# Turning q and k on VectorE and through HBM instead of on TensorE, in one encoder block on one core

## The chip, the core and the metric

The kernel runs on one NeuronCore of one Trainium2 chip. The metric is the device time of one execution in microseconds (us), lower is better. TensorE (PE in the profile, with its weight load PEld), VectorE (DVE), ScalarE (ACT) and GpSimd (POOL) each work through their own list of instructions in order; SyncE (SP) issues transfers. GpSimd issues transfers too. An instruction that waits holds up all that stand behind it on its engine.

## The reference

One layer of a bidirectional encoder, x of 512 tokens by 1024 features, float32. The tokens are a grid of 8 rows by 64 columns.

```python
x = x + 0.5 * swiglu1(rmsnorm(x))                    # 1024 -> 2 * 2816 -> 1024
h = rmsnorm(x)
xr, gr, q, k, v, ga, gb = split(h @ w_in)            # seven times 1024 columns
# A: depthwise conv of xr, two RG-LRU scans (forward, backward), summed, times gelu(gr)
q = rmsnorm(q per head, q_norm) * 64 ** -0.5         # 16 heads of 64
k = rmsnorm(k per head, k_norm)
s = q @ k^T + rel_pos_bias in a window of 8 rows x 16 columns   # -inf outside
B = softmax(s) @ v
x = x + (sigmoid(ga) * A + sigmoid(gb) * B) @ w_out
x = x + 0.5 * swiglu2(rmsnorm(x))
```

## The kernel before

**Layout.** The residual lies with features on partitions: eight tiles of 128 features by 512 tokens. Tokens are ordered by four column blocks of 16 columns, in each of them 8 rows of 16. Every product is made of three float32r matmuls (high times high, high times low, low times high): a weight tile of 128x1024 comes in on SP (`load_w`, L159), ACT rounds it to its high part (L145) and DVE subtracts to get the low part (L148). Three raw buffers and four pairs of high and low parts let the loads run ahead of TensorE.

**Stages.** The first feed-forward runs to about 330 us, the xr projection and the convolution follow, then q, k and v (`tok_group`, L822, tokens on partitions, in two halves of eight heads), the three gate projections (`gates`, L1070), the output projection (L1114) and the second feed-forward.

**What runs between.** The attention and the recurrence are written as generators in lanes (`lanes`, L574): `att` and `tail` hold attention, `lru` the recurrence, `v` the gathers of V. `weave(rate)` (L577) advances each lane by its rate of `RATE` (L83) at fixed places of the projections. The rates in the gate stage are "g". A scheduler of the language then sets each engine's order; `hold` (L251) ties an instruction behind the last projection matmul issued at that place, as an order and not as a wait.

**q and k.** For each half, `qk_raw` (L838) leaves four tiles of q and four of k, tokens on partitions, and the sums of squares per head. `heads` (L896) turns the sums into inverse norms (L901, L903, L904), multiplies them in (L909) and then, in `start(fi)` for each of four groups of two heads, turns q and k to features on partitions by eight TensorE transposes against `ident` (L918, L920). ACT evicts q and k with the norm weights as scale (L924, L927), DVE makes the low parts (L926, L929).

**Scores and softmax.** `scores` (L933) makes 12 matmuls for each group and half of the column blocks (24 where both halves go together, in the second half). DVE adds the bias and takes the maximum (L970), ACT takes the exponent and the row sum (L977), DVE inverts the sum (L979) and multiplies it in (L982). `ship` (L985) turns the probabilities in 32x32 blocks on DVE (L991, L992), writes them to HBM on SP (`pd`, L994) and reads them back rearranged by four GpSimd transfers (`PT`, L998). `apply` (L1001) multiplies by V.

**V.** `v_get` (L852) writes V to HBM (`vd`, L860). `v_more` (L866) gathers what is shifted against the column blocks: three `vs` tiles (L869) and, for the two edge blocks, `va` and `ve` in twelve GpSimd transfers (L880). The first half's gathers are issued at once, the second half's advance with lane `v` at 0.25. `bm` tiles (L892) are the bias, on GpSimd as well.

Of the kernel before, what the change touches and what calls it, by code (L numbers as in the profile page):

```python
# [9 lines left out]
F32 = mybir.dt.float32  # L10
F32R = mybir.dt.float32r
AF = mybir.ActivationFunctionType
ALU = mybir.AluOpType
# [3 lines left out]
P = 128  # L17
# [9 lines left out]
NCB, QC = 4, 16  # L27
# [16 lines left out]
C_QN, C_KN = 112, 113  # L44
# [39 lines left out]
    "xr": {"att": 0.0, "lru": 2.75},  # L84
    "t0": {"att": 0.0, "lru": 3.25},
    "t1": {"att": 0.75, "tail": 0.75, "lru": 2},
    "g": {"att": 0.7, "tail": 0.7, "lru": 1.5, "v": 0.25},
}


# [1 line left out]
def block_kernel(ctx: ExitStack, tc, a, out):  # L92
    nc = tc.nc
# [7 lines left out]
    dram = ctx.enter_context(tc.tile_pool(name="dram", bufs=1, space=bass.MemoryType.DRAM))  # L101
# [4 lines left out]
    mark = {}  # L106

    def nm(s):
        uid[0] += 1
        return f"{s}_{uid[0]}"  # L110
# [3 lines left out]
    def big_t(dt=F32, shape=(P, T), n="b"):  # L114
        return big.tile(list(shape), dt, tag="big", bufs=NBIG, name=nm(n))
# [4 lines left out]
    def acc_t():  # L120
        return acc.tile([P, T], F32, tag="acc", name=nm("acc"))

    def aux_t():
        return aux.tile([P, T], F32, tag="aux", name=nm("aux"))


    small = const.tile([P, NSMALL], F32, name="small")
# [4 lines left out]
    ident = const.tile([P, P], F32, name="ident")  # L132
# [118 lines left out]
    def hold(i):  # L251

        after(i, mark["mm"])
        return i
# [316 lines left out]
        end(t1, o)  # L571


    lanes = {"att": [], "tail": [], "lru": [], "v": []}  # L574
    due = {"att": 0.0, "tail": 0.0, "lru": 0.0, "v": 0.0}

    def weave(rate):  # L577
        for ln, n in rate.items():
# [11 lines left out]
    def until(ln, done):  # L590
        while lanes[ln] and not done():
            weave({ln: 1.0})
# [63 lines left out]
    ab = const.tile([P, 16], F32, name="ab")  # L656
# [21 lines left out]
    nc.vector.tensor_scalar(sn8, sp, -8.0, None, ALU.mult)  # L678
    gq8 = const.tile([P, 1], F32, name="gq8")
    nc.vector.tensor_scalar(gq8, small[:, C_QN : C_QN + 1], HD**-0.5, None, ALU.mult)  # L680
    gk = small[:, C_KN : C_KN + 1]

    state = {}

    def perm(ap):

        return ap.rearrange("p (r j c) -> p j r c", r=ROWS, j=NCB)
# [150 lines left out]
    def qk_raw(w, hf, st):  # L838
        raws = []
        for ps in tok_group(w, hf):  # L840
            t = big_t(n="qk")
            with tc.high_priority():
                copy = nc.scalar.activation(t, ps, AF.Copy)
            raws.append(t)
        for j, t in enumerate(raws):
            sq = big_t(n="sq")
            after(nc.scalar.activation(sq, t, AF.Square), copy)
            nc.vector.reduce_sum(st[:, w, j, :], sq.rearrange("p (h d) -> p h d", d=HD), axis=AX.X)
        weave(RATE[phase[0]])
        return raws  # L850

    def v_get(hf):  # L852
        for j, ps in enumerate(tok_group(2, hf)):
            t = big_t(n="v")
            with tc.high_priority():
                nc.vector.tensor_scalar(t, ps, rcol[:, j : j + 1], None, ALU.mult)
            V[hf, 2 * j] = t

        for j in range(NCB):
            nc.sync.dma_start(vd[hf][:, j * QC : (j + 1) * QC, :], V[hf, 2 * j])  # L860
        lanes["v"].append(v_more(hf))
        if hf == 0:
            until("v", lambda: False)
        weave(RATE[phase[0]])
# [28 lines left out]
            if g == 0:  # L893
                after(ld, mark["xr"])

    def heads(hf, raws, st):  # L896

        rq = tiny.tile([P, 2, NCB, 8], F32, tag="rq", name=nm("rq"))
        for w in range(2):
# [6 lines left out]
        for w in range(2):  # L906
            for j in range(NCB):
                t = raws[w][j].rearrange("p (h d) -> p h d", d=HD)
                hold(nc.vector.tensor_tensor(t, t, rq[:, w, j, :].unsqueeze(2).to_broadcast([P, 8, HD]), ALU.mult))  # L909
            yield  # L910
        qk, rss, soft, PTs = {}, {}, {}, {}


        def start(fi):
            fs = slice(fi * P, (fi + 1) * P)
            pq, pk = aux_t(), aux_t()
            for j in range(NCB):
                hold(nc.tensor.transpose(pq[:, j * P : (j + 1) * P], raws[0][j][:, fs], ident))  # L918
            for j in range(NCB):
                hold(nc.tensor.transpose(perm(pk)[:, j], raws[1][j][:, fs], ident))  # L920
            rev = lambda t: t.rearrange("p (j t) -> p j t", j=NCB)[:, :, ::-1]
            fwd = lambda t: t.rearrange("p (j t) -> p j t", j=NCB)
            qh, ql, kh, kl = (big_t(F32R, n=n) for n in ("qh", "ql", "kh", "kl"))
            nc.scalar.activation(rev(qh), fwd(pq), AF.Copy, scale=gq8)  # L924
            with tc.high_priority():
                nc.vector.scalar_tensor_tensor(rev(ql), fwd(pq), gq8, rev(qh.bitcast(F32)), ALU.mult, ALU.subtract)  # L926
            nc.scalar.activation(kh, pk, AF.Copy, scale=gk)  # L927
            with tc.high_priority():
                mark["kl"] = nc.vector.scalar_tensor_tensor(kl, pk, gk, kh.bitcast(F32), ALU.mult, ALU.subtract)  # L929
            grid = lambda t: t.rearrange("p (r c) -> p r c", r=ROWS)  # L930
            qk[fi] = qh, ql, grid(kh), grid(kl)

        def scores(fi, n2s):  # L933

            qh, ql, kh, kl = qk[fi]
            if 0 in n2s:
                rss[fi] = tiny.tile([P, 2, NCB], F32, tag="rs", name=nm("rs"))
            rs = rss[fi]
            pss = {n2: [aux_t() if n2 == n2s[0] else acc_t() for _ in range(2)] for n2 in n2s}
            for n in [n2 * 2 + i for n2 in n2s for i in range(2)]:  # L940
                ps, i = pss[n // 2], n % 2
                if n in EDGE:
                    keys = lambda t: t[:, :, SSTART[n] : SSTART[n] + 2 * QC].rearrange("p r (g c) -> p g r c", c=8)
                else:
                    keys = lambda t: t[:, :, KSTART[n] : KSTART[n] + 2 * QC].rearrange("p r (h c) -> p h r c", h=2)
                cs = slice(i * 256, (i + 1) * 256)
                for q_, k_ in ((qh, kl), (qh, kh), (ql, kh)):
                    for hp in (1, 0):
                        o = slice(hp * HD, (hp + 1) * HD)
                        mm = hold(nc.tensor.matmul(  # L950
                            ps[hp][:, cs], q_[o, n * P : (n + 1) * P], keys(k_[o]),
                            start=k_ is kl, stop=q_ is ql))
            for n2 in n2s:

                soft[fi, n2] = big_t(n="p"), big_t(n="p")
            for n2, hp in [(n2, hp) for n2 in n2s for hp in range(2)]:
                ps = pss[n2]
                bm = bms[hf * 4 + fi, hp]
                so = big_t(n="so")
                nmx = tiny.tile([P, 2], F32, tag="nmx", bufs=4, name=nm("nmx"))  # L960
                parts = []
                for i in range(2):
                    n = n2 * 2 + i
                    w = BIAS[n].stop - BIAS[n].start
                    pt = soft[fi, n2][n not in EDGE][:, hp * w : (hp + 1) * w]
                    parts.append(pt)
                    so_ = so[:, i * 256 : i * 256 + w]
                    o = i * 256 + (ROWS * (KSTART[n] - SSTART[n]) if n in EDGE else 0)
                    with tc.high_priority():
                        nc.vector.tensor_tensor_reduce(  # L970
                            so_, ps[hp][:, o : o + w], bm[:, BIAS[n]],
                            -1.0, 3.0e38, ALU.add, ALU.min, nmx[:, i : i + 1])
                    if n in EDGE and hp == (n == 0):

                        pt, so_ = (t.rearrange("p (g k) -> p g k", k=G) for t in (pt, so_))
                        pt = pt[:, ::-1]
                    nc.scalar.activation(pt, so_, AF.Exp, scale=-1.0, bias=nmx[:, i : i + 1],  # L977
                                         accum_out=rs[:, hp, n : n + 1])
                nc.vector.reciprocal(rs[:, hp, n2 * 2 : n2 * 2 + 2], rs[:, hp, n2 * 2 : n2 * 2 + 2])  # L979
                for i, pt in enumerate(parts):  # L980
                    n = n2 * 2 + i
                    nc.vector.tensor_scalar(pt, pt, rs[:, hp, n : n + 1], None, ALU.mult)  # L982
            return mm

        def ship(fi, n2):  # L985
# [73 lines left out]
    att = [None] * KT  # L1059
    phase = ["t0"]  # L1060
    bias(0)
    for hf in range(2):
        st = tiny.tile([P, 2, NCB, 8], F32, tag="st", name=nm("st"))
        raws = [qk_raw(0, hf, st), qk_raw(1, hf, st)]
        v_get(hf)
        lanes["att"].append(heads(hf, raws, st))
        phase[0] = "t1" if hf == 0 else "g"


# [144 lines left out]
```

## Time and profile before

| what | value |
|---|---|
| two runs | 1114.73 and 1115.2 us, median 1114.97 |
| the profiled execution | 1114.18 us |
| its span | 1112.4 us |
| mean granted TensorE clock | 0.997 |
| busy: PE, PEld, DVE, ACT, POOL | 1100.6, 974.8, 813.2, 578.0, 149.3 us |

The span is what the profile's time axis covers; some 1.8 us lie around it. Busy time is per engine and overlaps. A line such as "PE L918 MATMUL aux<-ident,qk x4" names the engine, the line of the kernel, the operation and the tiles by the program's names; in the time line "[4.72 <-DMA va<-vd]" is idle time ahead of the instruction and what ended it. "issue" means a wait for nothing that the profile shows.

### The profile page before, as it was taken

To read this page: it belongs to the slowest core of one execution; us is meant where nothing else is said; L and a number is where in the kernel's file an instruction comes from. 1 tells how busy PE (TensorE), PEld (TensorE's weight loads), DVE (VectorE), ACT (ScalarE), POOL (GpSimd) and SP (SyncE) were. 2 spreads that over 40 slices of the span, in tenths; PEclk is the share of its full clock that TensorE was granted. 3 is DMA by queue.
4 is the path that set the end of the run, shared out by engine and by line. 5 is a ranking of instruction groups with operands and counts; after the bars stand their busy time and mean duration, and the time that the engine had idled before them with its cause. 6 is when DMAs were issued, how large, how long until landed. Compare 5 with 4: busy or idle time off the path is not lost.

```text
span 1112.4 us, 17673 instructions
## 1 busy us (share of the span) xinstructions
PE 1100.6 (99%) x6811; PEld 974.8 (88%) x6811; DVE 813.2 (73%) x1295; ACT 578.0 (52%) x871; POOL 149.3 (13%) x243
## 2 busy tenths in 40 slices
PE   9999999999999999999999979999999999999998
PEld 8899999988888778788888868889999999998887
DVE  7878777794745776999877956759877777785542
ACT  8554544563533679877454432346554454564330
POOL 0000000000000351230333542001000000000000
PEclk9999999999999999999999989999999999999999
DMA  8566666643423685573687655377766666553421
GB/s 267 153 169 152 150 156 167 159 147 95 133 82 107 168 255 152 167 210 106 211 260 184 195 176 160 104 239 160 199 146 158 157 166 147 157 170 95 133 76 38
DMA packets 64548, 175.93 MB, mean 158 GB/s; under 512 B 14544, under 2 KB 18384, under 8 KB 64464
## 3 DMA queue, kind: packets, MB, share of 16 engines
q1 hardware_dynamic: 43136, 127.75, 35.5%
q0 software_dynamic: 20752, 46.80, 21.0%
q8 instruction: 53, 0.87, 0.3%
q10 hardware_dynamic: 576, 0.26, 0.1%
q14 instruction: 31, 0.25, 0.1%
HBM read 150.53 MB, written 15.73 MB: 149 GB/s over the span
## 4 chain that ended last, share of the span: by engine, by line
PE 95%; issue 1%; DMA 1%; DVE 1%; POOL 1%; ACT 0%; ACTq 0%; POOLq 0%
PE acc L312 31%; PE acc L172 10%; PE acc L173 10%; PE acc L174 10%; PE aux L312 5%; PE acc L831 4%; PE acc L832 4%; PE acc L833 4%; PE aux L174 4%; PE aux L172 4%; PE aux L173 4%; PE aux L742 1%; PE aux L1013 1%; PE aux L950 1%; PE acc L464 1%
## 5 line engine op out<-in xcount | busy, mean ns | idle before, releaser
L145 ACT ACTIVATE wh<-wraw 128x1024 fp32r<-128x1024 f32 (+3 forms) x224 | 220.3, 988 | 304.2 <-issue 95.0
L148 DVE TENSOR_TENSOR wl<-wraw,wh 128x1024 fp32r<-128x1024 f32 (+3 forms) x236 | 267.0, 1136 | 100.1 <-ACT wh L145 98.8
L312 PE MATMUL acc<-s,wh 128*128 128x256 f32 x1280 | 232.2, 283 | 0.0
L312 PEld LDWEIGHTS acc<-s,wh 128*128 128x128 f32 x1280 | 199.7, 192 | 0.0
L312 PE MATMUL acc<-s,wl 128*128 128x256 f32 x640 | 181.1, 283 | 0.0
L312 PEld LDWEIGHTS acc<-s,wl 128*128 128x128 f32 x640 | 122.9, 192 | 0.0
L172 PE MATMUL acc<-xh,wh 128*128 128x512 f32 x272 | 107.5, 395 | 0.0
L174 PE MATMUL acc<-xh,wl 128*128 128x512 f32 x272 | 106.2, 391 | 0.0
L173 PE MATMUL acc<-xl,wh 128*128 128x512 f32 x272 | 106.1, 390 | 0.0
L312 PE MATMUL acc<-xl,wh 128*128 128x256 f32 x320 | 90.6, 283 | 0.0
L312 PE MATMUL acc<-xh,wl 128*128 128x256 f32 x320 | 90.6, 283 | 0.0
L312 PE MATMUL acc<-xh,wh 128*128 128x256 f32 x320 | 90.5, 283 | 0.0
L831 PE MATMUL acc<-wh,xh 128*128 128x512 f32 x192 | 75.7, 394 | 0.0
L832 PE MATMUL acc<-wh,xl 128*128 128x512 f32 x192 | 74.8, 389 | 0.0
L833 PE MATMUL acc<-wl,xh 128*128 128x512 f32 x192 | 74.8, 389 | 0.0
L148 DVE TENSOR_TENSOR hl<-h,hh 128x512 fp32r<-128x512 f32 x88 | 57.2, 687 | 21.7 <-PE aux L173 21.5
L172 PE MATMUL aux<-hh,wh 128*128 128x512 f32 (+1 forms) x181 | 69.9, 386 | 0.0
L173 PE MATMUL aux<-hl,wh 128*128 128x512 f32 (+1 forms) x181 | 69.9, 386 | 0.0
L174 PE MATMUL aux<-hh,wl 128*128 128x512 f32 (+1 forms) x181 | 69.9, 386 | 0.0
L174 PE MATMUL acc<-hh,wl 128*128 128x512 f32 (+1 forms) x176 | 67.9, 386 | 0.0
L173 PE MATMUL acc<-hl,wh 128*128 128x512 f32 (+1 forms) x176 | 67.9, 386 | 0.0
L172 PE MATMUL acc<-hh,wh 128*128 128x512 f32 (+1 forms) x176 | 67.9, 386 | 0.0
(221 smaller groups left out, 2297.6 us busy)
## 6 DMA issues: line engine op xcount, KB each, us to landing
wraw<-wqkv SPq DMA_DIRECT2D x24, 512.0 KB, 4.5
wraw<-wg SPq DMA_DIRECT2D x24, 512.0 KB, 7.4
wraw<-w1d SPq DMA_DIRECT2D x22, 512.0 KB, 3.7
wraw<-w2s SPq DMA_DIRECT2D x22, 512.0 KB
pair<-w2s SPq DMA_DIRECT2D x22, 512.0 KB, 4.4
wraw<-w2d SPq DMA_DIRECT2D x22, 512.0 KB, 3.6
wraw<-w1s SPq DMA_DIRECT2D x18, 512.0 KB, 3.5
pair<-w1s SPq DMA_DIRECT2D x18, 512.0 KB, 4.7
```

The costliest lines, as they stand in the source:

```text
L145: nc.scalar.activation(H, raw, AF.Copy)
L148: return nc.vector.tensor_tensor(L, raw, H.bitcast(F32), ALU.subtract)
L172: nc.tensor.matmul(ps, wh, xh, start=first, stop=False, skip_group_check=skip)
L173: nc.tensor.matmul(ps, wh, xl, start=False, stop=False, skip_group_check=skip)
L174: mark["mm"] = nc.tensor.matmul(ps, wl, xh, start=False, stop=last, skip_group_check=skip)
L312: mm = nc.tensor.matmul(o, w_[:, c], x_, start=first and m + k == 0 and w_ is H and x_ is xh_, stop=m + k == 4 and w_ is L, skip_group_che ...
L464: nc.tensor.matmul(pre[i], w[i][1][:, s], xh[k], start=k == 0, stop=False)
L742: prev, mm = mm, nc.tensor.matmul(ps[d][b], W[w][o, c], X[x][o], start=x == 1, stop=w + x == 0)
L831: nc.tensor.matmul(pss[j], xh[kk][:, tj], H[:, s], start=kk == 0, stop=False)
L832: nc.tensor.matmul(pss[j], xl[kk][:, tj], H[:, s], start=False, stop=False)
L833: mark["mm"] = nc.tensor.matmul(pss[j], xh[kk][:, tj], L[:, s], start=False, stop=kk == KT - 1)
L950: mm = hold(nc.tensor.matmul(ps[hp][:, cs], q_[o, n * P : (n + 1) * P], keys(k_[o]), start=k_ is kl, stop=q_ is ql))
```

## The change

- **q and k are turned without TensorE.** `turn_qk` takes over the norm and its product. After the product, each of the eight tiles of a half is turned by one DVE `transpose` in 32x32 blocks into a tile `qkt`, and four GpSimd transfers write it to a tensor `qd` in HBM, 32x4 runs of 512 bytes each: 32 transfers a half. `heads` reads it back with `fetch(fi)` on SP, one transfer for q and one for k for each group, 128x16 runs of 128 bytes each. The loads for the next group are issued in `start`. The eight TensorE transposes of `start` are gone; ACT and DVE read the fetched tile in SBUF instead of PSUM. k_norm is folded into the scale of q.
- **The second half's turn is in a lane of its own**, `prep`, which advances at 0.25 in the gate stage; `heads` first empties it.
- **The inverse row sum is multiplied in by ACT** (an activation with a scale) instead of DVE.
- **Lane `v` advances at 0.5** in the gate stage instead of 0.25.

```diff
-    "g": {"att": 0.7, "tail": 0.7, "lru": 1.5, "v": 0.25},
+    "g": {"att": 0.7, "tail": 0.7, "lru": 1.5, "v": 0.5, "prep": 0.25},
...
-    def heads(hf, raws, st):
+    def turn_qk(raws, st, qd):
...
                 hold(nc.vector.tensor_tensor(t, t, rq[:, w, j, :].unsqueeze(2).to_broadcast([P, 8, HD]), ALU.mult))
-            yield
+                t2 = big_t(n="qkt")
+                nc.vector.transpose(
+                    t2.rearrange("p (c f i) -> p f c i", c=NCB, i=32), raws[w][j].rearrange("p (f c i) -> p f c i", c=NCB, i=32))
+                for ab in range(NCB):
+                    nc.gpsimd.dma_start(
+                        qd[w].rearrange("(c i) j a x -> j a i c x", c=NCB)[j, ab],
+                        t2[ab * 32 : (ab + 1) * 32].rearrange("p (c x) -> p c x", c=NCB))
+                if j % 2 == 1:
+                    yield
+
+    def heads(hf, qd):
+
+        xs = {}
+
+        def fetch(fi):
+            for w in range(2):
+                xs[w, fi] = big_t(n="xqk")
+                nc.sync.dma_start(
+                    xs[w, fi].rearrange("p (x i) -> p x i", i=32),
+                    qd[w].rearrange("p j a (f i) -> f p (j a) i", i=32)[fi])
+
+        until("prep", lambda: False)
+        fetch(0)
+        yield
...
-            pq, pk = aux_t(), aux_t()
-            for j in range(NCB):
-                hold(nc.tensor.transpose(pq[:, j * P : (j + 1) * P], raws[0][j][:, fs], ident))
-            for j in range(NCB):
-                hold(nc.tensor.transpose(perm(pk)[:, j], raws[1][j][:, fs], ident))
+            if fi < 3:
+                fetch(fi + 1)
+            xq, xk = (xs.pop((w, fi)).rearrange("p (j a i) -> p j a i", j=NCB, i=32) for w in range(2))
...
-            nc.scalar.activation(rev(qh), fwd(pq), AF.Copy, scale=gq8)
+            hold(nc.scalar.activation(rev(qh), xq, AF.Copy, scale=gq8))
...
-                    nc.vector.tensor_scalar(pt, pt, rs[:, hp, n : n + 1], None, ALU.mult)
+                    nc.scalar.activation(pt, pt, AF.Copy, scale=rs[:, hp, n : n + 1])
...
-        lanes["att"].append(heads(hf, raws, st))
+        lanes["att" if hf == 0 else "prep"].append(turn_qk(raws, st, qd))
+        lanes["att"].append(heads(hf, qd))
```

On TensorE, before, at the first group of the first half: eight transposes (L918 of q, L920 of k) between two stretches of the v projection (L831 to L833).

```order
L833 MATMUL acc_5122<-wl_5158,xh_3094 128x512
L918 MATMUL aux_5186<-ident,qk_4440 128x128
L918 MATMUL aux_5186<-ident,qk_4442 128x128
L918 MATMUL aux_5186<-ident,qk_4444 128x128
L918 MATMUL aux_5186<-ident,qk_4446 128x128
L920 MATMUL aux_5187<-ident,qk_4625 128x8x16
L920 MATMUL aux_5187<-ident,qk_4627 128x8x16
L920 MATMUL aux_5187<-ident,qk_4629 128x8x16
L920 MATMUL aux_5187<-ident,qk_4631 128x8x16
L831 MATMUL acc_5119<-wh_5207,xh_3096 128x512
```

On TensorE, now, at the first scores of the second half (L971 is the score matmul, kl_6382 and qh_6379 come from the first group that is fetched for that half):

```order
L172 MATMUL acc_6356<-xh_3102,wh_6358 128x512
L173 MATMUL acc_6356<-xl_3103,wh_6358 128x512
L174 MATMUL acc_6356<-xh_3102,wl_6359 128x512
L971 MATMUL aux_6402<-kl_6382,qh_6379 128x256
L971 MATMUL aux_6401<-kl_6382,qh_6379 128x256
L971 MATMUL aux_6402<-kh_6381,qh_6379 128x256
L971 MATMUL aux_6401<-kh_6381,qh_6379 128x256
L971 MATMUL aux_6402<-kh_6381,ql_6380 128x256
L971 MATMUL aux_6401<-kh_6381,ql_6380 128x256
```

No transposes are left. Counted in the order from the end of the last recurrence gates (L742) on, 312 projection matmuls now precede the first scores of the first half (216 before), and 600 precede the first scores of the second half (528 before).

On GpSimd, before, between the last probabilities of the first half and V's edges of the second (PT, bm, vs, va and ve as above, vd_82 is the second half's V):

```order
L998 DMA PT_5901<-pd_5899 128x1x224 x4
L892 DMA bm_6325<-rpb 128x640
L869 DMA vs_6018<-vd_82 128x1x512
L892 DMA bm_6327<-rpb 128x640
L869 DMA vs_6111<-vd_82 128x1x512
L998 DMA PT_6013<-pd_6011 128x1x224 x4
L892 DMA bm_6540<-rpb 128x640
L892 DMA bm_6542<-rpb 128x640
L876 MEMSET ve_6330 128x512
L880 DMA va_6329<-vd_82 64x4x64 x2
L880 DMA ve_6330<-vd_82 64x4x64
```

On GpSimd, now, the end of the same stretch; qd_5323 and qd_5324 are q and k of the second half, L1019 reads the probabilities back:

```order
L914 DMA qd_5323<-qkt_6056 32x4x128 x2
L914 DMA qd_5323<-qkt_6063 32x4x128 x4
L892 DMA bm_6133<-rpb 128x640
L892 DMA bm_6135<-rpb 128x640
L880 DMA va_6049<-vd_82 64x4x64 x2
L880 DMA ve_6050<-vd_82 64x4x64
L1019 DMA PT_6128<-pd_6126 128x1x224 x4
L914 DMA qd_5324<-qkt_6249 32x4x128 x4
L914 DMA qd_5324<-qkt_6256 32x4x128 x4
L1019 DMA PT_6243<-pd_6241 128x1x224 x4
L914 DMA qd_5324<-qkt_6326 32x4x128 x4
L914 DMA qd_5324<-qkt_6333 32x4x128 x4
```

The 32 writes of the second half's q and k stand among the first half's probabilities and the second half's V gathers; the last of them stand behind all eight groups of PT of the first half. V's edges of the second half, which stood behind all PT of the first half, now stand among them. From the first PT on to the last write of qd there are 32 transfers of PT, 32 of qd, 12 of va and ve, 3 of vs and 4 of bm.

On SP, now, at the second half's fetches (xqk):

```order
L163 DMA wraw_6945<-wg 128x1024
L1015 DMA pd_6241<-pt_6238 128x896
L163 DMA wraw_6977<-wg 128x1024
L927 DMA xqk_6339<-qd_5323 128x16x32
L927 DMA xqk_6341<-qd_5324 128x16x32
L927 DMA xqk_6375<-qd_5323 128x16x32
L927 DMA xqk_6377<-qd_5324 128x16x32
L927 DMA xqk_6489<-qd_5323 128x16x32
L1015 DMA pd_6472<-pt_6469 128x896
L927 DMA xqk_6491<-qd_5324 128x16x32
L1015 DMA pd_6482<-pt_6479 128x896
L163 DMA wraw_7117<-wg 128x1024
```

The fetches stand between the 18th and the 19th weight tile of the gate projections, and wait for all writes of qd.

More of the change, by code (lines that the diff above doesn't have):

```diff
@@ L571, in ffn @@
         end(t1, o)
-    lanes = {"att": [], "tail": [], "lru": [], "v": []}
-    due = {"att": 0.0, "tail": 0.0, "lru": 0.0, "v": 0.0}
+    lanes = {"att": [], "tail": [], "lru": [], "v": [], "prep": []}
+    due = {"att": 0.0, "tail": 0.0, "lru": 0.0, "v": 0.0, "prep": 0.0}
     def weave(rate):
@@ L680, in block_kernel @@
     nc.vector.tensor_scalar(gq8, small[:, C_QN : C_QN + 1], HD**-0.5, None, ALU.mult)
-    gk = small[:, C_KN : C_KN + 1]
+    nc.vector.tensor_tensor(gq8, gq8, small[:, C_KN : C_KN + 1], ALU.mult)
     state = {}
@@ L911, in heads @@
+                if j % 2 == 1:
[11 more added lines that the diff above has]
+        yield
         qk, rss, soft, PTs = {}, {}, {}, {}
         def start(fi):
-            fs = slice(fi * P, (fi + 1) * P)
@@ L916, in start @@
-            pq, pk = aux_t(), aux_t()
-            for j in range(NCB):
-                hold(nc.tensor.transpose(pq[:, j * P : (j + 1) * P], raws[0][j][:, fs], ident))
-            for j in range(NCB):
-                hold(nc.tensor.transpose(perm(pk)[:, j], raws[1][j][:, fs], ident))
-            rev = lambda t: t.rearrange("p (j t) -> p j t", j=NCB)[:, :, ::-1]
-            fwd = lambda t: t.rearrange("p (j t) -> p j t", j=NCB)
+            if fi < 3:
+                fetch(fi + 1)
+            xq, xk = (xs.pop((w, fi)).rearrange("p (j a i) -> p j a i", j=NCB, i=32) for w in range(2))
@@ L923, in start @@
+            xk = xk.rearrange("p j a (r c) -> p j a r c", r=2)
+            rev = lambda t: t.rearrange("p (j t) -> p j t", j=NCB)[:, :, ::-1].rearrange("p j (a i) -> p j a i", i=32)
+            rows = lambda t: t.rearrange("p (a r j c) -> p j a r c", a=NCB, r=2, j=NCB)
             qh, ql, kh, kl = (big_t(F32R, n=n) for n in ("qh", "ql", "kh", "kl"))
-            nc.scalar.activation(rev(qh), fwd(pq), AF.Copy, scale=gq8)
+            hold(nc.scalar.activation(rev(qh), xq, AF.Copy, scale=gq8))
@@ L925, in start @@
             with tc.high_priority():
-                nc.vector.scalar_tensor_tensor(rev(ql), fwd(pq), gq8, rev(qh.bitcast(F32)), ALU.mult, ALU.subtract)
-            nc.scalar.activation(kh, pk, AF.Copy, scale=gk)
+                nc.vector.scalar_tensor_tensor(rev(ql), xq, gq8, rev(qh.bitcast(F32)), ALU.mult, ALU.subtract)
+            hold(nc.scalar.activation(rows(kh), xk, AF.Copy))
             with tc.high_priority():
-                mark["kl"] = nc.vector.scalar_tensor_tensor(kl, pk, gk, kh.bitcast(F32), ALU.mult, ALU.subtract)
+                mark["kl"] = nc.vector.tensor_tensor(rows(kl), xk, rows(kh.bitcast(F32)), ALU.subtract)
@@ L1064, in block_kernel @@
         raws = [qk_raw(0, hf, st), qk_raw(1, hf, st)]
+        qd = [dram.tile([P, NCB, NCB, P], F32, tag="qd", bufs=4, name=nm("qd")) for _ in range(2)]
         v_get(hf)
-        lanes["att"].append(heads(hf, raws, st))
+        lanes["att" if hf == 0 else "prep"].append(turn_qk(raws, st, qd))
+        lanes["att"].append(heads(hf, qd))
         phase[0] = "t1" if hf == 0 else "g"
```

## The prediction, made before the run

> **What bounds the kernel now.** I read the busy times and the chain's shares first, then TensorE's waits, then the gate stage slice by slice (busy us and instructions of PE, PEld, DVE, ACT, POOL; granted clock, DMA share, GB/s).
>
> ```profile
> PE 1100.6 (99%) x6811; PEld 974.8 (88%) x6811; DVE 813.2 (73%) x1295; ACT 578.0 (52%) x871; POOL 149.3 (13%) x243
> PE 95%; issue 1%; DMA 1%; DVE 1%; POOL 1%; ACT 0%; ACTq 0%; POOLq 0%
> PE aux L1013 <- DMA va<-vd: 6.9, 2, 4.7
> 560.00:600.00 40.00, 40.00 (x219) 32.57 (x217) 32.20 (x81) 21.16 (x40) 16.58 (x25) 1.00 0.85 238
> 640.00:660.00 20.00, 13.01 (x71) 10.27 (x68) 9.26 (x31) 5.84 (x18) 9.33 (x14) 0.83 0.53 155
> ```
>
> TensorE is the bound, and it waits at one place: 6.9 us for V's edges, in the slice whose clock is 0.83. So only two things can shorten the run, TensorE's own instructions and this wait; every other edit counts only if it makes TensorE wait. That depends on the queues, so I read those next.
>
> **The wait for V's edges.** TensorE's time line through the first apply of the second half, and a block of the same size later, in which only three score-free stretches lie:
>
> ```profile
> 637.39 0.39 PE L174 MATMUL acc<-xh,wl 128*128 128x512 f32 x1
> ...
> 645.64 0.66 PE L1013 MATMUL aux<-PT,va 128*64 128x128 f32 x2 [4.72 <-DMA va<-vd]
> 648.49 0.44 PE L1013 MATMUL aux<-PT,va 128*64 128x128 f32 x1 [2.20 <-DMA va<-vd]
> 649.97 1.12 PE L918 MATMUL aux<-ident,qk 128*128 128x128 f32 x4
> ...
> 651.59 0.56 PE L172 MATMUL acc<-xh,wh 128*128 128x512 f32 x1
> ...
> 662.44 0.39 PE L174 MATMUL acc<-xh,wl 128*128 128x512 f32 x1
> 666.33 0.50 PE L172 MATMUL acc<-xh,wh 128*128 128x512 f32 x1
> ```
>
> From one L174 to the next L172 the stalled apply with its transposes takes 651.59 − 637.39 = 14.20 us, the later one without either 666.33 − 662.44 = 3.89. The difference, 10.3 us, is the stall, one set of transposes at a lowered clock and slow matmuls. With 0.79 us of it counted under transposes below, the wait costs 9.5. In the new order the edges stand among the first half's probabilities, long before their use: the 9.5 us go.
>
> **The transposes.**
>
> ```profile
> 508.99 0.60 PE L918 MATMUL aux<-ident,qk 128*128 128x128 f32 x4
> 509.42 0.60 PE L920 MATMUL aux<-ident,qk 128*128 128x128 f32 x4
> 509.78 0.48 PE L831 MATMUL acc<-wh,xh 128*128 128x512 f32 x1
> ```
>
> A start holds TensorE for 509.78 − 508.99 = 0.79 us; eight starts are 6.3 us, all on the path.
>
> **VectorE and ScalarE.**
>
> ```profile
> L982 DVE TENSOR_SCALAR p<-p,rs 128x256 f32<-128x256 f32 x32 | 11.4, 357 | 0.1
> L982 DVE TENSOR_SCALAR p<-p,rs 128x192 f32<-128x192 f32 x32 | 10.1, 316 | 0.2
> L992 DVE STREAM_TRANSPOSE pt<-p 128x512 f32<-128x512 f32 x16 | 11.0, 687 | 0.5 <-DMA pd<-pt 0.5
> L977 ACT ACTIVATE p<-so,nmx 128x256 f32<-128x256 f32 x32 | 15.9, 497 | 4.2 <-DVE nmx L970 4.1
> ```
>
> VectorE loses 11.4 + 10.1 = 21.5 us and gains 16 transposes of 0.687, 11.0 us. ScalarE gains 64 activations; bounded above by the exponent's 497 ns and below by the 316 ns of VectorE's multiply, 20 to 32 us; I take 30. In the 560 to 600 slice ScalarE is busy for 21.16 of 40 us, and TensorE for all of them. The cover is the weight split, which both do ahead of use; with it gone, each activation in a probability's chain would cost its half microsecond, at most 32 us in all. I price both at nothing.
>
> Up to here: 1114.2 − 9.5 − 6.3 = **1098.4**.
>
> **What the change adds to GpSimd's queue.** The probabilities, V's edges and now q and k pass through one queue in order. How it paces is in its time line and the landing times:
>
> ```profile
> 485.20 1.57 POOL L880 DMA_DIRECT2D va<-vd  x2
> 501.55 0.77 POOL L880 DMA_DIRECT2D ve<-vd  x1
> 528.16 2.02 POOL L998 DMA_DIRECT2D PT<-pd  x3 [25.84 <-DMA pd<-pt]
> 532.38 0.66 POOL L998 DMA_DIRECT2D PT<-pd  x1 [2.20 <-issue]
> ...
> 563.84 2.46 POOL L998 DMA_DIRECT2D PT<-pd  x3 [5.11 <-DMA pd<-pt]
> 591.21 0.66 POOL L998 DMA_DIRECT2D PT<-pd  x1 [0.21 <-issue]
> POOL PT L998 <- issue: 58.3, 33, 5.0
> PT<-pd POOLq DMA_DIRECT2D x64, 112.0 KB, 4.7
> L759 POOL DMA_DIRECT2D gate<-pair x64 | 32.9, 524 | 55.1 <-DVE gate L778 34.7 <-ACT pair L752 18.1 <-issue 1.4
> ```
>
> Three PT go out at 0.67 us each, the fourth waits 2.2 us though its source is there, and 58.3 us of the 64 PT's idle time have no releaser: the queue seems to take three of these and then wait until one has landed. From 563.84 to 591.87 the queue put out 16 PT and three small transfers, 28.0 us; less 1.8 for the three (the gate writes' 0.524, taken as 0.6), 1.64 us for a PT. Twelve va and ve took 485.20 to 502.3, 17.1 us, 1.43 each. A qd write of 64 KB has no row. Its nearest row is the gate write's 524 ns of issue (128 partitions, long runs); the upper end is va's 1.43. I take 0.6.
>
> From the first PT of the first half to the last qd of the second, the new order has 32 PT × 1.64 = 52.5, 12 va and ve × 1.43 = 17.1, 32 qd × 0.6 = 19.2, seven vs and bm × 0.6 = 4.2, together **93 us**, less some 3 where PT stand close to small ones: 90. At issue cost alone (0.67, 0.78, 0.524, 0.524) it is 21.4 + 9.4 + 16.8 + 3.7 = 51.3, and with memsets and gaps 57: the lower end. With 1.43 for qd it is 119.
>
> The Trainium skill prices this queue otherwise: "DMA: Bandwidth & Descriptors", section "Anatomy of one DMA — SWDGE (gpsimd) path", gives a GpSimd transfer about 2.0 us fixed plus its bytes at 436 GB/s, an estimate of 2.3 us for a PT of 112 KB; with three in flight that would be 0.77 us each and a queue near the lower end. The trace has 4.7 at the median, and the measurement decides.
>
> **When the queue starts and when TensorE arrives.**
>
> ```profile
> 515.41 0.39 PE L950 MATMUL aux<-kl,qh 64*128 64x256 f32 x2
> 605.49 0.39 PE L950 MATMUL aux<-kl,qh 64*128 64x256 f32 x2
> 465.33 0.50 PE L831 MATMUL acc<-wh,xh 128*128 128x512 f32 x1
> 508.75 0.40 PE L833 MATMUL acc<-wl,xh 128*128 128x512 f32 x1
> 546.45 4.40 SPq L860 DMA_DIRECT2D vd<-v  x4
> va<-vd POOLq DMA_DIRECT2D x16, 64.0 KB, 4.3
> pair<-x SPq DMA_DIRECT2D x16, 256.0 KB, 5.6
> L924 ACT ACTIVATE qh<-aux,gq 128x512 fp32r<-128x512 f32 x8 | 5.4, 673 | 2.3 <-PE aux L918 2.3
> ```
>
> 192 projection matmuls lie from 465.33 to the transposes at 508.99: 0.2274 us each. The first scores of the first half come 96 matmuls later, 21.8 us, less 0.79 for a start: 515.41 + 21.0 = 536.4. They may wait for the write and fetch of q and k; between nothing, since the 96 matmuls are there to cover the turn, and 10 us, a landing (4.3) and a fetch (5.6) laid bare; I take 2. The first PT stood 12.8 us behind the scores (528.16 − 515.41). Now the probabilities' turn comes behind the second scores and the write on SP behind the four vd writes of 4.40 us: 5.5 us more. So the first PT is at 536.4 + 2 + 18.3 = 557, the last qd issued at 557 + 90 = 647. It lands 4.3 later (va, as large), the fetch takes 5.6 (pair<-x, as large, in long runs), the evictions on ScalarE and VectorE 0.7 each: q and k are there at **658**.
>
> TensorE reaches these scores 72 matmuls later than before, 16.4 us, less five starts (4.0) and an apply that now comes after (1.1): 605.5 + 11.3 = **616.8**. It then waits 658 − 617 = **41 us**. With the queue at 57 us, 8; with 119, 70. The other applies and projections stand behind these scores on TensorE, so nothing covers it; the weights are there, since SP's fetch stands behind the eighteenth weight tile only, and the next tiles come while TensorE waits.
>
> After a long wait the clock is low: the four transposes at 649.97 took 1.12 us, those at 508.99 0.60. I add 2 us. The fetches of 128-byte runs have no row either. The nearest transfers of small packets are in a window with nothing else:
>
> ```profile
> DMA packets 383, 0.37 MB, mean 306 GB/s; under 512 B 46, under 2 KB 362, under 8 KB 383
> q1 hardware_dynamic: 383, 0.37, 93.1%
> ```
>
> 383 packets of about 1 KB took 93.1% of 16 engines for 1.2 us (the window 9.8 to 11), 47 ns each. A fetch is 2048 runs, 128 on each engine: 6 us if a short packet takes as long, 0.8 if only its bytes count. Only the first fetch of each half is exposed; the 5.6 above is near the upper end. The skill speaks for that end, and against the change: "DMA: Bandwidth & Descriptors", section "Specifications", says that line rate needs 512 bytes and that smaller pieces are read, modified and written. By that the sum would be some 6 us longer for each first fetch.
>
> Sum: 1098.4 + 41 + 2 (first half's scores) + 2 (clock) = 1143.4; the profiled run is 0.8 below the median, so 1144, and with a microsecond for weight splits started late, **1145**.
>
> **The rivals.** *The queue holds the second half's scores* (the forecast): for it speak 58.3 us of unexplained idle time on PT and the place of the last qd behind all PT. With waits of 27 to 58 us, 1128 to 1161. Chance 0.57.
>
> *The queue clears in time:* if the landings were slow because the queue's transfers met the weights' (0.85 DMA share in 560 to 600), small qd writes in between fill the gaps where PT waits, and the 83 transfers take 50 to 68 us instead of 90. The wait is then 0 to 20 us, and the time 1098 to 1119. Against it: three in flight also where the queue had been empty, at 528.16. It decides at about 49 us of queue for no wait at all (617 − 11.3 − 557), 65 us for the time of before. A wait of 20 to 27 is shared with the forecast. Chance 0.25.
>
> *The short runs are slow:* each run of 128 bytes costs more than a 1 KB packet and the four fetches contend with weights; then each half's first scores wait another 6 to 20 us, on top of the queue: 1150 to 1180. Nothing in the profile has runs that short on SP. Chance 0.13.
>
> *The change doesn't do what it says:* V's edges are still late, since they too stand behind slow PT, and the 9.5 us stay; but the wait for the scores then comes ahead of that apply and covers it. Only without the queue's wait does it count: 1108 to 1115, chance 0.05.
>
> **How the numbers follow.** 2% of the time, about what a measurement can tell, is 1092.7 to 1137.3. Faster than 1092.7 would need more than TensorE's 15.8 us and no new wait: 0.02, from the second rival. Within: nearly all of that rival and the last, and the part of the forecast with a wait under 33 us, 0.10: 0.39. Slower: the rest, 0.59. The range leaves out a tenth at each end: 1106 to 1167. The forecast's own range is 1128 to 1161.
>
> **What would show it.** Right: TensorE idle by some 40 us at its first L971 of the second half, ended by q's or k's eviction behind xqk; a granted clock well below 1 in that slice; GpSimd with the last qd (L914) after 640; no va wait at L1034. Wrong: qd writes that go out at half a microsecond with PT under 1 us each (the queue isn't held by landings); a wait at the first half's scores longer than 10 us (the fetch, or the turn, is slow); projections that wait for wl or wh (ScalarE or VectorE has become late).

## The result, and the profile after

The changed kernel takes 1147.5 us (median of two runs, 1147.45 and 1147.62) against 1114.97: a ratio of 1.0287, 95% interval 1.0271 to 1.0304. It is slower, by 32.6 us. The profiled execution took 1147.62 us, its span is 1145.8 us.

The page of the changed kernel, busy times and the chain's shares:

```profile
PE 1095.6 (96%) x6747; PEld 969.7 (85%) x6747; DVE 805.8 (70%) x1248; ACT 607.2 (53%) x938; POOL 184.1 (16%) x307
PE 93%; POOL 3%; issue 2%; DMA 1%; ACT 1%; DVE 0%; DVEq 0%; SPq 0%; POOLq 0%
```

TensorE is busy for 5.0 us less than before (1100.6), and idle for 50.2 us (1145.8 − 1095.6) instead of 11.8. The difference of the idle times, 38.4, less the 5.0, is the 33.4 us by which the span grew. GpSimd's transfers, which had 1% of the chain, have 3%. The waits of TensorE name where:

```profile
PE aux L971 <- DVE kl L950: 41.5, 1, 41.5
PE acc L172 <- DVE v L856: 2.7, 1, 2.7
PE acc L831 <- ACT qk L843: 1.2, 1, 1.2
```

L971 is the score matmul. One wait of 41.5 us holds nearly everything; the wait for V's edges, 6.9 us before, is gone. The slices (columns as before: PE, PEld, DVE, ACT, POOL, clock, DMA share, GB/s) show TensorE standing still, and in the second of them every other engine but GpSimd too:

```profile
620.00:640.00 20.00, 1.72 (x8) 1.10 (x6) 11.96 (x19) 3.13 (x5) 10.38 (x16) 0.60 0.75 204
640.00:660.00 20.00, 0.00 (x0) 0.00 (x0) 0.00 (x0) 0.00 (x0) 13.31 (x23) 0.50 0.50 129
```

The granted clock falls to 0.50. The Trainium skill has this ("TensorE: Matmul & The Clock Gate", Part 1: half clock after some 3.4 us without work); the 0.50 agrees. The trace of this kernel shows the clock lower behind a shorter wait too, of 2.7 us (time line under "Why the prediction was right").

The chain through this wait, in order of time (start, duration), ends at the scores at 663.19:

```profile
651.65 1.35 POOL qd L914 x3
...
653.34 2.18 POOL qd L914 x4
655.52 1.92 DMA qd<-qkt
...
657.66 4.09 DMA xqk<-qd
...
661.78 0.64 ACT kh L948
...
662.44 0.70 DVE kl L950
```

It is the chain that the prediction walked: last write of k in GpSimd's queue, its landing (1.9 us), the fetch's (4.1), ScalarE's eviction, VectorE's. GpSimd's time line at both ends of the stretch:

```profile
562.44 2.20 POOL L1019 DMA_DIRECT2D PT<-pd  x3 [10.20 <-DMA pd<-pt]
568.35 0.67 POOL L1019 DMA_DIRECT2D PT<-pd  x1 [3.70 <-issue]
...
651.64 4.43 POOL L914 DMA_DIRECT2D qd<-qkt  x8
```

Its waits (us in total, times, longest):

```profile
POOL PT L1019 <- issue: 58.7, 32, 4.2
```

The group of the qd writes (busy and mean ns, then idle time before them):

```profile
L914 POOL DMA_DIRECT2D qd<-qkt x64 | 35.2, 560 | 5.3 <-DVE qkt L911 5.1 <-issue 0.2
```

Again three PT go out at once and the fourth waits. A qd write holds the queue for 0.560 us. From the first PT to the end of the last qd write 93.6 us pass (562.44 to 656.07). The landings:

```profile
PT<-pd POOLq DMA_DIRECT2D x64, 112.0 KB, 5.0
qd<-qkt POOLq DMA_DIRECT2D x64, 64.0 KB, 2.9
xqk<-qd SPq DMA_DIRECT2D x16, 256.0 KB, 5.6
```

### The profile page after: what moved, and what is told of

The parts are those of the page before. It is cut to its first block, busy times and chain, and to the rows that moved or that the text cites. A ratio compares the mean times of both kernels' runs of the same rounds, so it can differ in the third digit from the quotient of the medians.

```text
span 1145.8 us, 17689 instructions
## 1 busy us (share of the span) xinstructions
PE 1095.6 (96%) x6747; PEld 969.7 (85%) x6747; DVE 805.8 (70%) x1248; ACT 607.2 (53%) x938; POOL 184.1 (16%) x307
## 4 chain that ended last, share of the span: by engine, by line
PE 93%; POOL 3%; issue 2%; DMA 1%; ACT 1%; DVE 0%; DVEq 0%; SPq 0%; POOLq 0%
PE acc L312 30%; PE acc L172 10%; PE acc L173 10%; PE acc L174 10%; PE aux L312 5%; PE acc L831 4%; PE acc L832 4%; PE acc L833 4%; PE aux L172 4%; PE aux L174 4%; PE aux L173 4%; PE aux L1034 1%; PE aux L742 1%; POOL qd L914 1%; PE aux L971 1%
## 5 line engine op out<-in xcount | busy, mean ns | idle before, releaser
L831 PE MATMUL acc<-wh,xh 128*128 128x512 f32 x192 | 75.2, 393 | 1.2 <-ACT qk L843 1.2
L833 PE MATMUL acc<-wl,xh 128*128 128x512 f32 x192 | 74.7, 389 | 0.0
```

The source lines that it names most:

```text
L831: nc.tensor.matmul(pss[j], xh[kk][:, tj], H[:, s], start=kk == 0, stop=False)
L833: mark["mm"] = nc.tensor.matmul(pss[j], xh[kk][:, tj], L[:, s], start=False, stop=kk == KT - 1)
```

## The experiments

All ratios are against the kernel before, run on the same chip in turns with it.

| run | time, us | ratio, 95% interval | wait at the second half's first scores, us |
|---|---|---|---|
| the change | 1147.5 | 1.0287 (1.0271 to 1.0304) | 41.5 |
| 3072 bytes | 1133.2 | 1.0155 (1.0136 to 1.0175) | 26.8 |
| 4096 bytes | 1130.2 | 1.0137 (1.0110 to 1.0164) | 21.4 |
| qd of the second half on SP | 1122.1 | 1.0071 (1.0054 to 1.0088) | 15.9 |
| turn at rate 1.0 | 1129.9 | 1.0144 (1.0112 to 1.0177) | 19.3 |
| second half reads old q and k | 1132.1 | 1.0154 (1.0135 to 1.0172) | 17.1 |
| SP and rate 0.5 | 1117.6 | 1.0026 (1.0016 to 1.0036) | none |
| SP, rate 0.5, 4096 bytes | 1108.7 | 0.9946 (0.9931 to 0.9961) | 3.2 |
| before, lane v at 0.5 | 1109.0 | 0.9947 (0.9927 to 0.9966) | none |
| before, ScalarE's product | 1131.1 | 1.0144 (1.0129 to 1.0159) | none |
| before, both of these | 1109.1 | 0.9950 (0.9938 to 0.9962) | none |
| before, both, 4096 bytes | 1108.6 | 0.9941 (0.9929 to 0.9952) | none |
| before, lane v at 0.5, 4096 bytes | 1104.3 | 0.9905 (0.9892 to 0.9917) | none |

Only the change itself lies more than 2% from the kernel before. The other differences are smaller, but each interval leaves out 1. Waits are of one profiled execution, times are medians of two to eleven.

**Does the queue hold the scores, and what limits it? More descriptor space.** The theory: GpSimd's queue takes about three PT and waits for a landing. The rival: the landings are slow by themselves. The builder's argument below sets how much space the kernel keeps for describing GpSimd's transfers. Only this size is changed, and no engine's order.

```diff
-    nc = bacc.Bacc("TRN2", ..., dynamic_dma_scratch_size=2048)
+    nc = bacc.Bacc("TRN2", ..., dynamic_dma_scratch_size=3072)
```

> The changed kernel with 3072 bytes of descriptor space for GpSimd's transfers instead of 2048; every engine's instructions stay in the same order. Queue theory (about three PT in flight, the next waits for a landing): four or five in flight, PT at about 1.0 us each where they were 1.64, the last qd write some 20 us earlier than 656, TensorE's wait at the second half's first scores 41.5 -> about 20 us, time about 1126. Rival (landings are slow because the transfers share engines with the weights, so more in flight only makes each slower): pace, wait and time stay, 1147.

The run with 3072 bytes, GpSimd's time line at its first PT, which now go out four at once:

```profile
562.58 2.87 POOL L1019 DMA_DIRECT2D PT<-pd  x4 [10.40 <-DMA pd<-pt]
```

The waits of GpSimd and TensorE:

```profile
POOL PT L1019 <- issue: 11.2, 6, 3.6
PE aux L971 <- DVE kl L950: 26.8, 1, 26.8
```

And the landing of PT:

```profile
PT<-pd POOLq DMA_DIRECT2D x64, 112.0 KB, 5.4
```

The unexplained idle time ahead of PT falls from 58.7 to 11.2 us, with 4096 bytes (below) it has no row any more. The landings are at 5.4 us at the median where they were at 5.0, so with more in flight each became little slower. The wait falls by 14.7 us, the time by 14.4. The rival, by which nothing would change, is out; the gain was smaller than the 21 us expected.

```diff
-    nc = bacc.Bacc("TRN2", ..., dynamic_dma_scratch_size=2048)
+    nc = bacc.Bacc("TRN2", ..., dynamic_dma_scratch_size=4096)
...
-        rq = tiny.tile([P, 2, NCB, 8], F32, tag="rq", name=nm("rq"))
+        rq = tiny.tile([P, 2, NCB, 8], F32, tag="rq", bufs=1, name=nm("rq"))
```

> The same with 4096 bytes (and one buffer instead of two for the inverse norms, to make room). Queue theory: about seven in flight, PT near their issue cost of 0.67 us; what then sets the last qd is the last probabilities' write to HBM (624) with 4 PT and 8 qd behind it. Wait 5 to 20 us, time 1110 to 1126, I expect 1117. Rival: 1147, landings of PT rise from 5.0 us to about 10.

The second edit, one buffer instead of two for the inverse norms (`rq`), comes with 4096 bytes in all four kernels that have them; no run has it alone.

The waits of GpSimd and TensorE in the run with 4096 bytes, where PT land in 5.0 us at the median, and GpSimd's last qd writes:

```profile
POOL qd L914 <- DVE qkt L911: 11.8, 4, 4.6
PE aux L971 <- DVE kl L950: 21.4, 1, 21.4
626.36 2.23 POOL L914 DMA_DIRECT2D qd<-qkt  x4 [2.28 <-DVE qkt L911]
...
631.53 4.69 POOL L914 DMA_DIRECT2D qd<-qkt  x8 [0.22 <-issue]
```

With 1130 us I missed the range. The queue's pace is no longer the limit: now it waits 11.8 us for VectorE's turned tiles (5.1 in the change), and the last writes end at 636.2 where they ended at 656.1. Behind the queue's 20 us stood a second lateness of 21. The lines point to the turn's place in the orders, late on VectorE and with the last eight writes behind four more PT on GpSimd; the next runs test that.

**Is it the qd writes' place behind PT?** The second half's qd writes go out on SP; the first half's stay on GpSimd.

```diff
-                    nc.gpsimd.dma_start(
+                    (nc.sync if phase[0] == "g" else nc.gpsimd).dma_start(
                         qd[w].rearrange("(c i) j a x -> j a i c x", c=NCB)[j, ab],
```

> The changed kernel with the second half's 32 qd writes issued by SP instead of GpSimd; TensorE's order is the same. Queue theory: the qd writes no longer stand behind PT; q and k are there when VectorE has turned them, the wait falls from 41.5 to about 10 us, time about 1114 (1103 to 1125). If the fetches' short runs were the cause: the wait stays over 30 us, time over 1136. If SP's own queue holds the writes behind weight loads: between.

TensorE's time line at its first scores of the second half, and SP's ahead of it:

```profile
636.12 0.58 PE L971 MATMUL aux<-kl,qh 64*128 64x256 f32 x2 [15.87 <-DVE kl L950]
618.19 5.52 SPq L914 DMA_DIRECT2D qd<-qkt  x8
623.76 0.55 SPq L927 DMA_DIRECT2D xqk<-qd  x1
624.40 4.24 SPq L163 DMA_DIRECT2D wraw<-wg  x1
628.87 9.22 SPq L927 DMA_DIRECT2D xqk<-qd  x4
```

The wait falls by 25.6 us, the time by 25.5. The 15.9 that remain are the last turned tiles (written from 618.19 on), and k's fetch, which at 624.40 stands behind a weight load. TensorE is there at 620.3 (636.12 − 15.87).

**The turn earlier, still on GpSimd.**

```diff
-    "g": {..., "v": 0.5, "prep": 0.25},
+    "g": {..., "v": 0.5, "prep": 1.0},
```

> The changed kernel with the second half's turn at rate 1.0 instead of 0.25: its qd writes stand ahead of the last 20 PT of the first half instead of behind all 32. Queue theory: the wait at the second half's first scores goes (0 to 3 us), and PT of the first half come some 17 us later, which their applies may wait for by a few us; time about 1102 (1098 to 1112). If place in the queue doesn't matter (fetch or landing is slow by itself): 1140 or more.

SP's time line at the second half's first fetches in this run:

```profile
627.87 0.33 SPq L1015 DMA_DIRECT2D pd<-pt  x1
628.50 0.52 SPq L927 DMA_DIRECT2D xqk<-qd  x1
630.26 2.03 SPq L1015 DMA_DIRECT2D pd<-pt  x1
633.01 12.66 SPq L927 DMA_DIRECT2D xqk<-qd  x4
```

GpSimd's last qd write in it:

```profile
603.56 0.55 POOL L914 DMA_DIRECT2D qd<-qkt  x1 [0.59 <-DMA bm<-rpb]
```

It goes out 52 us earlier, and the wait is still 19.3 us: a plain miss of my expectation. The order on SP places q's fetch behind the write of the first half's last probabilities but one, which waits until 627.87 for VectorE's turn of them, and k's fetch behind the write of the last (630.26). So an early q and k is not enough: the fetch's own place counts.

**No need for the new q and k at all.** The second half's fetches read the first half's tensors.

```diff
-        lanes["att"].append(heads(hf, qd))
+        qds.append(qd)
+        lanes["att"].append(heads(hf, qds[0]))
```

> The changed kernel, but the second half's fetches read the first half's q and k in HBM, which have long landed; the second half's turn and its 32 writes stay in GpSimd's queue, only nobody waits for them. So the scores of the second half are those of other heads. If only the wait for q and k cost time: 1101 to 1105. Queue theory: the queue ends at 645 to 656 all the same, and the second half's first PT stand behind it; their first apply comes some 36 us behind its scores, at about 658, and PT land at about 670, so that TensorE waits 8 to 15 us there instead: 1108 to 1120, I expect 1113.

The time lines of VectorE, SP and TensorE in this run:

```profile
627.18 1.18 DVE L148 TENSOR_TENSOR wl<-wraw,wh 128x1024 fp32r<-128x1024 f32 x1
628.39 0.33 SPq L163 DMA_DIRECT2D wraw<-wg  x1
628.77 13.40 SPq L927 DMA_DIRECT2D xqk<-qd  x5
640.03 0.58 PE L971 MATMUL aux<-kl,qh 64*128 64x256 f32 x2 [17.10 <-DVE kl L950]
```

I had expected the scores to pass and the applies to wait 8 to 15 us. It was the other way: the fetch is issued only at 628.77, behind a weight load that waits for VectorE's split of an earlier tile (until 628.36), and lands and is evicted by 640; PT then cost 1.8 us in all, and the scores of a later group wait 3.2. So of the 41.5 us some 17 are left when nobody needs the new q and k; by the time lines they come from the fetch's place on SP. The other 24 are the wait for the queue. VectorE itself is late there in part through the queue: the bias step, whose tile shares its buffers with the turned tiles, waits for a qd write. In the changed kernel's time line of VectorE, with the idle time and what ended it:

```profile
610.39 0.36 DVE L991 CUSTOM_DVE_ANT_0 so<-aux,bm 128x192 f32<-128x192 f32 x1 [6.70 <-DMA qd<-qkt]
```

How much of the 17 this makes was not tried by itself.

**Both places mended: SP and rate 0.5.**

```diff
-    "g": {..., "v": 0.5, "prep": 0.25},
+    "g": {..., "v": 0.5, "prep": 0.5},
...
-                    nc.gpsimd.dma_start(
+                    (nc.sync if phase[0] == "g" else nc.gpsimd).dma_start(
```

> The changed kernel with the second half's qd writes on SP and its turn at rate 0.5 instead of 0.25, so that the writes and the fetch stand ahead of the last probabilities on SP as well; TensorE's order is that of the changed kernel. Queue theory: q and k are there before TensorE is (the last turn comes some 20 us earlier than in the run with SP at 0.25), the 41.5 us wait is gone, and what is left is the prediction's sum without it, 1098.4, with the 2.7 us that TensorE waits for VectorE's eviction of v: time about 1102 (1099 to 1108). If the wait has another cause beside the queue and the turn's place, over 1112.

The waits of TensorE and GpSimd in this run:

```profile
PE aux L1034 <- DMA PT<-pd: 7.4, 2, 5.2
PE aux L1034 <- issue: 3.6, 1, 3.6
POOL PT L1019 <- issue: 75.0, 34, 5.8
```

The wait at the scores, 15.9 us, is gone, but the time falls by only 4.5 (1122.1 to 1117.6, where 1102 was expected): the next consumer, the applies (L1034), now waits 11.0 us for PT. The profiled execution was the longest of this kernel's runs (1122.9, median 1117.6), so these 11.0 are at the upper end. The queue is still full: V's edges, at 0.5, stand ahead of the first half's last PT. Its pace is the cause if space mends it:

```diff
-    nc = bacc.Bacc("TRN2", ..., dynamic_dma_scratch_size=2048)
+    nc = bacc.Bacc("TRN2", ..., dynamic_dma_scratch_size=4096)
...
-        rq = tiny.tile([P, 2, NCB, 8], F32, tag="rq", name=nm("rq"))
+        rq = tiny.tile([P, 2, NCB, 8], F32, tag="rq", bufs=1, name=nm("rq"))
```

> The run with the second half's qd writes on SP at rate 0.5, now with 4096 bytes of descriptor space; the order on every engine is the same. Queue theory: the 11.0 us that its applies wait for PT come from the queue's pace, so they go, and what is left is near the sum without the new wait: about 1104 (1100 to 1109). If PT land late for want of bandwidth: 1116 to 1118 as before.

The waits of TensorE in the run with this space:

```profile
PE aux L971 <- DVE kl L950: 3.2, 1, 3.2
PE acc L172 <- DVE v L856: 2.7, 1, 2.7
PE acc L831 <- ACT qk L843: 1.2, 1, 1.2
```

It does: no wait for PT is left, and 1117.6 becomes 1108.7, a little faster than the kernel before (0.9946). Waits of 3.2 + 2.7 + 1.2 us keep it from 1104.

**The other parts alone, on the kernel before.** Lane v:

```diff
-    "g": {"att": 0.7, "tail": 0.7, "lru": 1.5, "v": 0.25},
+    "g": {"att": 0.7, "tail": 0.7, "lru": 1.5, "v": 0.5},
```

> The kernel before with lane v at 0.5 in the gate stage, nothing else. V's edges of the second half stand ahead of the last 12 PT of the first half. Prediction's term: the 6.9 us wait and the low clock behind it go, 9.5 us: 1105.5 (1104 to 1109). Rival: PT of the first half's last groups come later and their applies wait instead: 1112 or more.

1109.0, a gain of 5.9 us where 9.5 were priced. V's edges are in time; the applies now wait for PT instead, 1.7 us in the profiled execution (1107.0); the runs spread from 1105 to 1113.

ScalarE's product, alone:

```diff
-                    nc.vector.tensor_scalar(pt, pt, rs[:, hp, n : n + 1], None, ALU.mult)
+                    nc.scalar.activation(pt, pt, AF.Copy, scale=rs[:, hp, n : n + 1])
```

> The kernel before with the inverse row sum multiplied in by ScalarE instead of VectorE, nothing else. Prediction's term: nothing, 1114 to 1116, since both lie beside TensorE's work. Rival: ScalarE's 64 activations hold up evictions or weight splits: 1118 or more.

The waits of TensorE in this run:

```profile
PE aux L1013 <- DMA va<-vd: 18.3, 3, 8.3
PE acc L831 <- ACT qk L843: 2.1, 1, 2.1
```

It costs 16 us, which I had priced at nothing. But 11.4 of them are a longer wait for V's edges (6.9 before): with the product on ScalarE the scheduler puts 8 more PT ahead of the last edge in GpSimd's queue (48 instead of 40; my expectation for the next run says 12 more, which is wrong). If so, lane v at 0.5 takes it away:

```diff
-    "g": {"att": 0.7, "tail": 0.7, "lru": 1.5, "v": 0.25},
+    "g": {"att": 0.7, "tail": 0.7, "lru": 1.5, "v": 0.5},
...
-                    nc.vector.tensor_scalar(pt, pt, rs[:, hp, n : n + 1], None, ALU.mult)
+                    nc.scalar.activation(pt, pt, AF.Copy, scale=rs[:, hp, n : n + 1])
```

> The kernel before with lane v at 0.5 and the inverse sum on ScalarE. The run with ScalarE alone took 1131, with 18.3 us of waits for V's edges, which had come to stand behind 12 more PT in GpSimd's queue. Queue theory: with the edges ahead of those PT this goes, and ScalarE's own time costs nothing: 1107 to 1111, as lane v alone. Rival: the 64 activations themselves cost 16 us: 1122 to 1126.

1109.1, the same as lane v alone: most of the 16 us were the queue's. ScalarE's own part is hidden here, since TensorE waits 2.1 us for the eviction of q and k behind activations, but 0.2 for PT instead of 1.7. With 4096 bytes, where the queue is nearly out of the way, it shows, with the product on ScalarE and without:

```diff
-    nc = bacc.Bacc("TRN2", ..., dynamic_dma_scratch_size=2048)
+    nc = bacc.Bacc("TRN2", ..., dynamic_dma_scratch_size=4096)
...
-        rq = tiny.tile([P, 2, NCB, 8], F32, tag="rq", name=nm("rq"))
+        rq = tiny.tile([P, 2, NCB, 8], F32, tag="rq", bufs=1, name=nm("rq"))
```

> The same with 4096 bytes. Queue theory: 1105 to 1108, within 2 us of the same without ScalarE's part. Rival: 1118 or more.

> The kernel before with lane v at 0.5 and 4096 bytes; its order is that of the run with lane v alone. That run kept 1.7 us of waits for PT at the applies; with the queue faster they go: 1105 to 1107.

1108.6 with the product on ScalarE (just over its range), 1104.3 without (just under its range): 4.2 us, of which 2.1 are that wait; the rest has no row of its own. The 1104.3 is the best version found, ratio 0.9905 (0.9892 to 0.9917): the kernel before, lane v at 0.5, and twice the descriptor space. In its profile no wait for V's edges or PT is left.

## Why the prediction was right, step by step

- **The wait itself**: 1145 us were forecast and 1147.5 came; 41 us were predicted at the second half's first scores, 41.5 came, and by the chain that was named. That the two waits agree so closely is in part luck. TensorE arrived 4.9 us later than forecast (621.7 for 616.8) and q and k were there 5 us later (663.1 for 658), which cancelled. The 5 us are themselves what is left of four misses: the first PT 5.4 us late (562.4 for 557), the queue 3.6 longer, the landing 2.4 shorter (1.92 for 4.3) and the fetch 1.5 shorter (4.09 for 5.6).
- **The queue's length**: 90 us predicted, 93.6 measured. The qd write at 0.6 was 0.560; three PT in flight was right, and the runs with more space show it as the cause, which the prediction could only infer from idle time without a releaser. The rival *queue clears in time* fails there: small writes in between did not lift the pace.
- **One cause too few.** The prediction took the queue as the only thing late. The run with old q and k shows 17 us at the same place from the fetch's place on SP. The step that failed is a missing term: the chain goes from q's and k's landing to the fetch with nothing in between, and "SP's fetch stands behind the eighteenth weight tile only" is looked at for TensorE's weights alone. These were there (no row of TensorE waits for wh or wl), but the weight load ahead of the fetch waits for VectorE, and the fetch with it. The number survived because the two run side by side, and the queue was the longer. Forecasts for mending that rest on the queue alone come out too good, and four expectations above did, by 13 to 28 us.
- **Short runs slow**, the third rival: not seen. The fetch of 128-byte runs landed in 5.6 us at the median, as the long runs of equal size did before (5.6), and in 4.1 on the chain. The 6 us that the prediction weighed against the change for short runs do not show here; no run has the same fetch in long runs.
- **V's wait, 9.5 us**: gone in the changed kernel. Lane v alone gains 5.9 us; with twice the descriptor space the two gain 10.9 (1115.2 to 1104.3). The term stands only where the PT behind the edges don't become late for it.
- **The transposes, 6.3 us**: no run has them alone. The nearest pair, both with 4096 bytes, v at 0.5 and ScalarE's product, is 1108.7 without them and 1108.6 with them: TensorE is busy 3.3 us less in the profiles (1096.2 against 1099.5), and what the turn adds in waits (2.7 for VectorE's eviction of v, 3.2 for kl) takes it back.
- **ScalarE and VectorE at nothing** failed twice. In the changed kernel TensorE waits 2.7 us for VectorE's eviction of v and 1.2 for ScalarE's of q and k. The v eviction stands behind ql, a weight split and kl of the second start, as VectorE's time line of the changed kernel shows:

```profile
544.56 0.75 DVE L947 SCALAR_TENSOR_TENSOR ql<-xqk,gq,qh 128x512 fp32r<-128x512 f32 x1
545.22 1.22 DVE L148 TENSOR_TENSOR wl<-wraw,wh 128x1024 fp32r<-128x1024 f32 x1
546.36 0.69 DVE L950 TENSOR_TENSOR kl<-xqk,kh 128x512 fp32r<-128x512 f32 x1
546.96 2.72 DVE L856 TENSOR_SCALAR v<-acc,rcol 128x512 f32<-128x512 f32 x4
```

  TensorE's time line behind this wait:

```profile
547.76 0.50 PE L172 MATMUL acc<-xh,wh 128*128 128x512 f32 x1 [2.70 <-DVE v L856]
...
548.83 0.63 PE L173 MATMUL acc<-xl,wh 128*128 128x512 f32 x1
```

  The wait for v comes in every run with the turn and in none without. From 548.83 to 552.21 the matmuls then start 0.43 us apart instead of 0.23, which costs some 1.7 us more. The two waits of 3.9 us and this cover the 4.9 by which TensorE was late. The cover that was named, weight splits, was the wrong one to look at: TensorE waited for evictions that free its accumulators, and the sum has no term for them.
- **First half's scores**: 2 us allowed; they came at 537.46 for 536.4, without a wait of their own. **Low clock**: 2 us allowed; TensorE's busy time fell by 5.0 us, where the transposes (6.3) and the slow matmuls around V's wait (10.3 − 6.9 − 0.8 = 2.6) went, 8.9; so by this estimate the clock cost some 4. By the starts of the matmuls it was about 2.2 behind the long wait, as allowed (24 score and 5 projection matmuls take 5.1 us from 663.19 on, an estimated 2.9 at full pace), and the 1.7 behind the wait for v, which was not.

## What to carry to other kernels

The queue that put out three transfers and then paused without a releaser was here out of descriptor space, and more space is a cheap test of that; its pace, and not its busy share (16% here), prices what is added to it. Where an operand is sent through memory, follow each hop with what stands ahead of it in its own queue: the write behind PT, the fetch behind a weight load, the eviction behind other evictions; mending one shows the next, some 5 to 20 us further on. And a product moved from one engine to another cost 16 us, most of it because the scheduler then ordered a third queue differently, so compare every engine's order, not the moved instruction's.

## What the runs showed of the hardware

In the changed kernel the unexplained waits ahead of PT went from 58.7 us to 11.2 and to none with 2048, 3072 and 4096 bytes of descriptor space, while the landing of a PT stayed at 5.0 to 5.4 us at the median (the longest went from 7.4 to 11.1): the chip had room for more transfers in flight than the kernel gave it. In the kernel before with lane v at 0.5, twice the space took these waits from 53.0 to 6.2 us and the median landing from 4.6 to 5.4, so more in flight was not quite free. The Trainium skill's price for a GpSimd transfer ("DMA: Bandwidth & Descriptors", section "Anatomy of one DMA — SWDGE (gpsimd) path", about 2.0 us and the bytes at 436 GB/s) would be an estimate of 2.15 us for a qd write, and the one at the end of the chain took 1.92, the median 2.9; for a PT it would be 2.3, where the trace has 5.0 at the median.
